# Stores of the up projection on the GpSimd queue, chunks of act in three pieces, the last normalisations in stages

## The chip, the cores and the metric

The kernel runs on one core of a Trainium2 chip. The metric is the device time of one execution in microseconds; less is better. The engines are TensorE (PE, matmul), VectorE (DVE), ScalarE (ACT) and GpSimd (POOL); SP is the queue that issues most DMAs.

## The reference

One layer of a hybrid encoder over 2048 tokens of width 1024, in float32: four mixers on a common input projection, an output projection with a residual and a layer normalisation, then a gated MLP with a causal convolution over 3 tokens, again with residual and normalisation. The change lies in the MLP and the last normalisation.

```python
def conv_ffn(h, w_up, conv_w, conv_b, w_down):            # D_FF = 2816
    u, gate = jnp.split(h @ w_up, 2, axis=-1)
    u = jax.nn.gelu(causal_dwconv(u, conv_w, conv_b))
    return (u * gate) @ w_down
...
    h = layer_norm(DN_ALPHA * h + y @ w_out[l], ln1_g[l], ln1_b[l])
    h = layer_norm(DN_ALPHA * h + conv_ffn(...), ln2_g[l], ln2_b[l])
```

## The kernel before

Every float32 operand of a matmul is split in a high and a low part, and a product is three matmuls: high by high (line 145), high by low (146 or 147) and low by high. The split of a tile is a cast on ScalarE (line 105) and a subtraction on VectorE (line 108). In the MLP the products of 2 by 2 blocks are taken as seven products of sums of blocks (numbered 1 to 7) in place of eight.

**Output projection** (`phase_o`): 16 tiles of 128 tokens. The layer normalisation of a tile (`layer_norm`, lines 80 to 94) runs over VectorE (statistics 85, 87, 91, product with the gain 93), GpSimd (reciprocal root 77 and 78, sum with the bias 94) and ScalarE (92); line 187 transposes the result on TensorE, lines 199, 200 and 219 are other work of GpSimd there.

**Up projection** (`phase_u`): 44 units, `fb` (half of the tokens) by `f` (128 of the 2816 channels), seven products of 12 matmuls each. In the first half the weights `wr` and their sums are stored in DRAM (`keep_sums`, line 1473, `su_d`, four a unit) and read back in the second half. `down_sums` makes sums of the down projection's weights and stores them (line 1505, `wt_d`). `activate` makes the convolution, the GELU and the gate (lines 1517 to 1523, tile `cv`, two buffers) and after each second unit four sums of blocks (`S`, one buffer), and stores `cv` and `S` to `ad_d`, 14 stores of 128 KB a pair of units (line 1537). All these stores are issued from SP, which also issues the loads of the weights.

**Down projection** (`phase_d`): the seven products in the order `DNO` (1, 6, 2, 5, 3, 7, 4), each over four chunks of act, 28 chunks in all. `load_b` loads the 11 weight tiles of a product (`dbr`, three buffers, line 1624; or straight into `db`) and splits them. `load_a` loads a chunk of act, 128 x 2816 (`da`, two buffers, 1408 KB, line 1632), and splits it as a whole, one chunk ahead of its use. A chunk gives two tiles of 33 matmuls; line 1674 adds the result to `accx` or `accy`. A tile of the output is complete with product 3 (`accx`) or 4 (`accy`): `residual` adds the residual (line 1639, `hres`), `finish` normalises in `layer_norm` and stores. For even tiles line 94 is on GpSimd, for odd ones on VectorE (`FL2`).

The instructions of each engine are put in order at build time by a scheduler that goes by the order of the code and by when buffers come free; on the chip each engine and each queue runs its own list in that order, and a waiting instruction holds up all that stand behind it.

Of the kernel before, what the change touches and what calls it, by code (L numbers as in the profile page):

```python
# [17 lines left out]
D = 1024  # L18
# [19 lines left out]
def r32(ap):  # L38
    return ap.bitcast(F32)
# [1372 lines left out]
def phase_u(K_, early):  # L1412
# [22 lines left out]
    with tc.tile_pool(name="uw", bufs=1, reuse_waits="tile", side="right") as ww, \  # L1435
# [35 lines left out]
        def keep_sums(n):  # L1471
            for q, i in enumerate((6, 5, 7, 3)):
                nc.sync.dma_start(K_.su_d[units[n][1], q], raws[n][i])

# [17 lines left out]
        def down_sums(j):  # L1492
            t = w.tile([128, 8, 256], F32, tag="wds", bufs=1, name="wds")
            for c in range(0, 512, 256):
                if c:
                    t = w.tile([128, 8, 256], F32, tag="wds", bufs=1, name="wds")
                for e in range(2):
                    nc.sync.dma_start(t[:, 2 * e:2 * e + 2], w_dn[j, e][:, :, c:c + 256])
                b11, b12, b21, b22 = (t[:, n] for n in range(4))
                t1, t2, t3, t4 = (t[:, 4 + n] for n in range(4))  # L1500
                V(t1, b12, b11, op=ALU.subtract)
                V(t2, b22, t1, op=ALU.subtract)
                V(t3, b22, b12, op=ALU.subtract)
                V(t4, b21, t2, op=ALU.subtract)
                nc.sync.dma_start(K_.wt_d[:, :, j, c:c + 256].rearrange("t p c -> p t c"), t[:, 4:8])
                yield
# [4 lines left out]
        def activate(n):  # L1511
# [13 lines left out]
            if f % 2:  # L1525
# [9 lines left out]
                for i, t in ((1, a11), (2, a12), (4, a22), (5, s1), (6, s2), (7, s3), (3, s4)):  # L1535
                    for c in range(2):
                        nc.sync.dma_start(K_.ad_d[i - 1, fb, c, :, j, :].rearrange("p (n c) -> p n c", c=128), t[:, 2 * c:2 * c + 2, :])

# [57 lines left out]
def phase_d(K_, out):  # L1596
# [12 lines left out]
    with tc.tile_pool(name="db", bufs=DBB, reuse_waits="tile") as wb, tc.tile_pool(name="dy", bufs=1, reuse_waits="tile") as cy, \  # L1609
# [19 lines left out]
        def load_a(i, fb, ch):  # L1629
            t = wa.tile([128, 2, NFP, 256], F32R, tag="da", name="da")  # L1630
            h, l = t[:, 0], t[:, 1]
            nc.sync.dma_start(r32(l), K_.ad_d[i - 1, fb, ch])
            K_.split(h, l, r32(l))
            return h, l

        def residual(ti, t):
# [3 lines left out]

        def finish(ti, t):
            K_.layer_norm(w, t, t, g2, b2, t, e2=nc.vector if FL2(ti) else None)
            nc.sync.dma_start(out[0, ti * 128:ti * 128 + 128, :], t)

# [9 lines left out]
        for s, (i, fb, ch) in enumerate(steps):  # L1654
# [7 lines left out]
            for t in range(2):  # L1662
# [16 lines left out]
                if i == 7:  # L1679
                    residual(ti + 1, y)  # L1680
                if i == 4:
                    finish(ti + 1, y)
            if later:
                ti, x = later.pop(0)
                residual(ti, x)
                finish(ti, x)

# [90 lines left out]
OBQ, OE2 = (lambda nc: nc.sync), (lambda nc, t: None)  # L1778
FL2 = lambda t: t % 2 == 1
FCB = 3  # L1780
# [37 lines left out]
```

## Time and profile before

| | |
|---|---|
| runs before | 3045.21 us median of 3 (3044.72 to 3049.33) |
| profiled execution | 3049.67 us, of which the span is 3047.9 us, mean granted TensorE clock 0.957 |
| busy share of the span | PE 92%, DVE 66%, ACT 41%, POOL 22% |
| instructions | PE 15515, DVE 3163, ACT 2017, POOL 534 |

The output projection runs from some 1495 to 1737 us of the profiled span, the up projection to 2580, the down projection from 2598 to 3034; the rest is the last normalisations. Busy shares are means over stages of very different kind, so each stage is read by itself.

### The profile page before, as it was taken

The numbers are of one execution on the slowest core, as the hardware profiler recorded it, in microseconds if no ns is written. First come the engines' busy times: TensorE is split into PE (matmuls) and PEld (weight loads), VectorE is DVE, ScalarE is ACT, GpSimd is POOL, SyncE is SP. The second block draws the span as 40 slices with busy tenths as digits, with TensorE's granted clock in tenths as the row PEclk, the third lists the DMA queues.
The fourth block names the chain that finished last, engine by engine and source line by source line (L and its number), as shares of the span: only waits on it lengthen the run. The fifth ranks groups of instructions, "written<-read, shape, count | busy, mean of one in ns | idle before, by whom it ended". The sixth has DMA issues, their size and how long they took to land. (4 is left out here: it accounts for less than half of the span.)

```text
span 3047.9 us, 42090 instructions
## 1 busy us (share of the span) xinstructions
PE 2793.5 (92%) x15515; PEld 2216.1 (73%) x15515; DVE 2013.2 (66%) x3163; ACT 1234.6 (41%) x2017; POOL 672.3 (22%) x534
## 2 busy tenths in 40 slices
PE   5899888999999877889888999999999998999997
PEld 3677766767677666777667788888888886788786
DVE  7877547555556286988866587787755556434666
ACT  3234233434433264555433354444644444332232
POOL 3433232222221252444445300000000000000111
PEclk8999997999999987999999999999999999999999
DMA  6566654646353456120566577775744443543462
GB/s 199 150 192 195 197 162 112 179 109 181 97 161 76 104 147 141 53 53 18 170 205 207 195 230 237 234 236 163 241 144 144 145 145 124 206 152 133 164 232 114
DMA packets 523757, 483.60 MB, mean 159 GB/s; under 512 B 100048, under 2 KB 432720, under 8 KB 517152
## 3 DMA queue, kind: packets, MB, share of 16 engines
q1 hardware_dynamic: 521584, 480.77, 51.8%
q8 instruction: 122, 2.00, 0.3%
q14 instruction: 83, 0.68, 0.1%
q10 hardware_dynamic: 1744, 0.14, 0.0%
q0 software_dynamic: 224, 0.01, 0.0%
HBM read 310.18 MB, written 170.64 MB: 158 GB/s over the span
## 5 line engine op out<-in xcount | busy, mean ns | idle before, releaser
L145 PE MATMUL u_ps<-bh,wh 128*128 128x512 f32 x1232 | 482.7, 392 | 6.2 <-ACT g L1581 3.2
L146 PE MATMUL u_ps<-bl,wh 128*128 128x512 f32 x1232 | 482.0, 391 | 0.0
L147 PE MATMUL u_ps<-bh,wl 128*128 128x512 f32 x1232 | 480.0, 390 | 0.6 <-DVE wl L1482 0.6
L137 POOL TENSOR_TENSOR wcl<-wraw,wch 128x512 fp32r<-128x512 f32 (+1 forms) x152 | 247.5, 1639 | 448.1 <-ACT wch L134 416.2
L1481 ACT CAST wh<-wr 128x512 fp32r<-128x512 f32 x308 | 189.7, 620 | 314.9 <-PE u_ps L146 270.6
L77 POOL TENSOR_SCALAR rsq_t<-ln_mv 128x1 f32<-128x1 f32 x48 | 19.2, 401 | 1334.2 <-DVE ln_mv L87 1293.1
L1482 DVE TENSOR_TENSOR wl<-wr,wh 128x512 fp32r<-128x512 f32 x308 | 210.8, 689 | 118.6 <-ACT wh L1481 118.6
L145 PEld LDWEIGHTS u_ps<-bh,wh 128*128 128x128 f32 x1232 | 231.5, 188 | 60.4 <-ACT g L1581 6.5
L147 PEld LDWEIGHTS u_ps<-bh,wl 128*128 128x128 f32 x1232 | 231.6, 188 | 51.7 <-DVE wl L1482 1.5
L146 PEld LDWEIGHTS u_ps<-bl,wh 128*128 128x128 f32 x1232 | 231.9, 188 | 47.8
L496 POOL TENSOR_TENSOR be<-be,af 128x512 f32<-128x512 f32 (+3 forms) x120 | 170.6, 1434 | 215.6 <-DVE af L494 129.3
L134 ACT CAST wch<-wraw 128x512 fp32r<-128x512 f32 (+1 forms) x152 | 110.2, 731 | 261.6 <-PE m L146 135.5
L145 PE MATMUL m<-hT,wch 128*128 128x512 f32 x448 | 190.3, 426 | 3.6 <-ACT wch L134 2.5
L147 PE MATMUL m<-hT,wcl 128*128 128x512 f32 x448 | 184.9, 413 | 2.6 <-POOL wcl L137 2.6
L146 PE MATMUL m<-hT,wch 128*128 128x512 f32 x448 | 184.6, 413 | 0.0
L494 DVE TENSOR_TENSOR_SCAN af<-sb_stay,af,sb_zero 128x513 f32<-128x513 f32 x96 | 137.6, 1450 | 7.3 <-ACT sb_stay L487 5.8
L146 PE MATMUL m<-hTl,wch 128*128 128x512 f32 x320 | 130.0, 406 | 8.1 <-POOL hTl L299 6.9
L145 PE MATMUL m<-hTh,wch 128*128 128x512 f32 x320 | 127.2, 404 | 6.9 <-DVE rw_halo L333 6.9
L105 ACT CAST da<-da 128x2816 fp32r<-128x2816 f32 x28 | 71.5, 2554 | 147.5 <-DMA da<-ad_d 141.7
L487 ACT ACTIVATE sb_stay<-a 128x512 f32<-128x512 f32 (+3 forms) x160 | 86.3, 539 | 110.8 <-PE a L483 63.5
L147 PE MATMUL m<-hTh,wcl 128*128 128x512 f32 x320 | 126.7, 396 | 0.0
L503 PE MATMUL b<-ident,be 128*128 128x128 f32 x544 | 92.6, 294 | 35.8 <-DVE wt L508 28.4
(516 smaller groups left out, 6383.5 us busy)
## 6 DMA issues: line engine op xcount, KB each, us to landing
wr<-in_ffn_w_up_dram SPq DMA_DIRECT2D x154, 256.0 KB
da<-ad_d SPq DMA_DIRECT2D x28, 1408.0 KB
wraw<-in_w_in_dram SPq DMA_DIRECT2D x112, 256.0 KB
su_d<-wr SPq DMA_DIRECT2D x88, 256.0 KB
ad_d<-S SPq DMA_DIRECT2D x176, 128.0 KB
wr<-su_d SPq DMA_DIRECT2D x88, 256.0 KB
wraw<-in_w_in_dram SPq DMA_DIRECT2D x40, 512.0 KB
ad_d<-cv SPq DMA_DIRECT2D x132, 128.0 KB
```

The costliest lines, as they stand in the source:

```text
L105: nc.scalar.copy(hi, src)
L134: nc.scalar.copy(hi[:, kk, cs], raw)
L137: (lo_eng or nc.vector).tensor_tensor(lo[:, kk, cs], raw, r32(hi[:, kk, cs]), op=ALU.subtract)
L145: nc.tensor.matmul(ps, lh, rh, start=start and i == 0, stop=False, **kw)
L146: nc.tensor.matmul(ps, lh, rl, start=False, stop=False, **kw)
L147: nc.tensor.matmul(ps, ll, rh, start=False, stop=i == n - 1, **kw)
L487: nc.scalar.activation(r[:, ns], lgn, AF.Sigmoid, scale=-1.0)
L494: nc.vector.tensor_tensor_scan(af[:, back], r[:, back], zero.to_broadcast([128, n + 1]), p["af"][:, TB - p["n"]:TB - p["n"] + 1] if p else ...
L496: (nc.gpsimd if i % 4 in WPP else nc.vector).tensor_tensor(be[:, ns], be[:, ns], af[:, TB - n + 1:], op=ALU.mult)
L503: nc.tensor.transpose(p[:, j * 128:(j + 1) * 128], u["be"][:, TB - n + j * 128:TB - n + (j + 1) * 128], K_.ident)
L1481: nc.scalar.copy(h, r)
L1482: V(l, r, r32(h), op=ALU.subtract)
```

## The change

All stores of the up projection go from SP to the queue of GpSimd. `load_a` loads and splits a chunk in three pieces of 4, 4 and 3 weight rows of 256 columns (1024, 1024 and 768 columns). `finish` becomes a generator of four stages, one taken after each tile of matmuls (`turn`); its statistics are instructions of their own (`stats`), of which one half of a tile is taken as soon as that half is final; line 94's sum is always on VectorE (now line 1667), and the very last tile runs in two halves, its store too.

```diff
@@ -1470,7 +1470,7 @@
 
         def keep_sums(n):
             for q, i in enumerate((6, 5, 7, 3)):
-                nc.sync.dma_start(K_.su_d[units[n][1], q], raws[n][i])
+                nc.gpsimd.dma_start(K_.su_d[units[n][1], q], raws[n][i])
 
         def weight(n, i):
             if n >= N:
@@ -1502,7 +1502,7 @@
                 V(t2, b22, t1, op=ALU.subtract)
                 V(t3, b22, b12, op=ALU.subtract)
                 V(t4, b21, t2, op=ALU.subtract)
-                nc.sync.dma_start(K_.wt_d[:, :, j, c:c + 256].rearrange("t p c -> p t c"), t[:, 4:8])
+                nc.gpsimd.dma_start(K_.wt_d[:, :, j, c:c + 256].rearrange("t p c -> p t c"), t[:, 4:8])
                 yield
 
         acts, stores = [], []
@@ -1534,7 +1534,7 @@
                 V(s4, a12, s2, op=ALU.subtract)
                 for i, t in ((1, a11), (2, a12), (4, a22), (5, s1), (6, s2), (7, s3), (3, s4)):
                     for c in range(2):
-                        nc.sync.dma_start(K_.ad_d[i - 1, fb, c, :, j, :].rearrange("p (n c) -> p n c", c=128), t[:, 2 * c:2 * c + 2, :])
+                        nc.gpsimd.dma_start(K_.ad_d[i - 1, fb, c, :, j, :].rearrange("p (n c) -> p n c", c=128), t[:, 2 * c:2 * c + 2, :])
 
         for i in (1, 2):
             moving(i, 0)
@@ -1629,18 +1629,54 @@
         def load_a(i, fb, ch):
             t = wa.tile([128, 2, NFP, 256], F32R, tag="da", name="da")
             h, l = t[:, 0], t[:, 1]
-            nc.sync.dma_start(r32(l), K_.ad_d[i - 1, fb, ch])
-            K_.split(h, l, r32(l))
+            for j in range(0, NFP, 4):
+                js = slice(j, min(j + 4, NFP))
+                nc.sync.dma_start(r32(l[:, js]), K_.ad_d[i - 1, fb, ch, :, js])
+                K_.split(h[:, js], l[:, js], r32(l[:, js]))
             return h, l
+
+        sts = {}
+
+        def stats(ti, t, q):
+            if ti not in sts:
+                sts[ti] = w.tile([128, 2, 6], F32, tag="ln_st", bufs=10, name="ln_st")
+            nc.vector.bn_stats(sts[ti][:, q, :], t[:, q * 512:(q + 1) * 512])
 
         def residual(ti, t):
             h = w.tile([128, D], F32, tag="hres", bufs=3, name="hres")
             nc.sync.dma_start(h, K_.h1_d[ti * 128:ti * 128 + 128, :])
             STT(t, h, ALPHA, t, op0=ALU.mult, op1=ALU.add)
 
-        def finish(ti, t):
-            K_.layer_norm(w, t, t, g2, b2, t, e2=nc.vector if FL2(ti) else None)
-            nc.sync.dma_start(out[0, ti * 128:ti * 128 + 128, :], t)
+        def finish(ti, t, last=False):
+
+            mv = w.tile([128, 2], F32, tag="ln_mv", bufs=3, name="ln_mv")
+            nc.vector.bn_aggr(mv, sts.pop(ti))
+            rs = w.tile([128, 1], F32, tag="ln_rs", bufs=3, name="ln_rs")
+            K_.rsqrt(w, rs, mv[:, 1:2], LN_EPS)
+            yield
+            nm = w.tile([128, 1], F32, tag="ln_nm", bufs=3, name="ln_nm")
+            STT(nm, mv[:, 0:1], -1.0, rs, op0=ALU.mult, op1=ALU.mult)
+            hs = [slice(0, 512), slice(512, D)] if last else [slice(0, D)]
+            for q in hs:
+                nc.scalar.activation(t[:, q], t[:, q], AF.Identity, scale=rs, bias=nm)
+            yield
+            for q in hs:
+                V(t[:, q], t[:, q], g2[:, q], op=ALU.mult)
+            yield
+            for q in hs:
+                V(t[:, q], t[:, q], b2[:, q], op=ALU.add)
+                nc.sync.dma_start(out[0, ti * 128:ti * 128 + 128, q], t[:, q])
+
+        run = []
+
+        def turn(new=None):
+
+            for r in list(run):
+                if next(r, 0) == 0:
+                    run.remove(r)
+            if new is not None:
+                next(new)
+                run.append(new)
 
         Bn = load_b(DNO[0])
         An = load_a(DNO[0], 0, 0)
@@ -1678,12 +1714,20 @@
                     later.append((ti, x))
                 if i == 7:
                     residual(ti + 1, y)
+                    stats(ti + 1, y, 1)
                 if i == 4:
-                    finish(ti + 1, y)
-            if later:
-                ti, x = later.pop(0)
-                residual(ti, x)
-                finish(ti, x)
+                    stats(ti + 1, y, 0)
+                    turn(finish(ti + 1, y, s + 1 == len(steps) and t))
+                elif t and later:
+                    ti, x = later.pop(0)
+                    residual(ti, x)
+                    stats(ti, x, 0)
+                    stats(ti, x, 1)
+                    turn(finish(ti, x))
+                else:
+                    turn()
+        while run:
+            turn()
 
 
 @with_exitstack
@@ -1776,7 +1820,6 @@
 
 
 OBQ, OE2 = (lambda nc: nc.sync), (lambda nc, t: None)
-FL2 = lambda t: t % 2 == 1
 FCB = 3
 DBB = 17
 QSTEP = 5
```

In the new listing line 1632 (load of `da`) is 1634, 1638 and 1639 are 1647 and 1648, 1643 (store of the output) is 1668, and 1674 is 1710; of the last normalisations 85 is 1643 (`stats`), 87 is 1653, 91 is 1658, 92 is 1661, 93 is 1664.

The SP queue at the end of the up projection, where the difference of the two orders is shown (`ad_d` is act in DRAM, `cv` and `S` the last unit's tiles, `dbr` the first weights of the down projection):

```order
-L1537 DMA ad_d<-cv 128x2x128 x2
-L1537 DMA ad_d<-S 128x256 x2
-L1632 DMA da<-ad_d 128x2816 x2
-L1537 DMA ad_d<-cv 128x2x128 x4
-L1537 DMA ad_d<-S 128x256 x6
-L1638 DMA hres<-h_d 128x1024 x2
+L1634 DMA da<-ad_d 128x1024 x2
+L1634 DMA da<-ad_d 128x768
+L1634 DMA da<-ad_d 128x1024 x2
+L1634 DMA da<-ad_d 128x768
+L1647 DMA hres<-h_d 128x1024 x3
 L1624 DMA dbr<-in_ffn_w_down_dram 128x512 x3
```

The stores are gone, and the loads of two chunks and three residuals stand directly ahead of the first `dbr`.

VectorE at the same place, from the last sum of products of the up projection on, before the change:

```order
L1578 TENSOR_TENSOR u<-u,u_ps 128x4x128
L1519 SCALAR_TENSOR_TENSOR cv<-u,ffn_cw,cv 128x1024 x2
L1523 TENSOR_TENSOR cv<-cv,g 128x1024
L1531 TENSOR_TENSOR S<-cv 128x512
L1532 TENSOR_TENSOR S<-S,cv 128x512
L1534 TENSOR_TENSOR S<-cv,S 128x512
L108 TENSOR_TENSOR da<-da 128x2816 x2
L108 TENSOR_TENSOR db<-dbr,db 128x512 x11
```

And in the changed kernel:

```order
L1578 TENSOR_TENSOR u<-u,u_ps 128x4x128
L1519 SCALAR_TENSOR_TENSOR cv<-u,ffn_cw,cv 128x1024 x2
L108 TENSOR_TENSOR da<-da 128x1024
L1523 TENSOR_TENSOR cv<-cv,g 128x1024
L108 TENSOR_TENSOR da<-da 128x1024
L1531 TENSOR_TENSOR S<-cv 128x512
L108 TENSOR_TENSOR da<-da 128x768
L1532 TENSOR_TENSOR S<-S,cv 128x512
L108 TENSOR_TENSOR da<-da 128x1024
L1534 TENSOR_TENSOR S<-cv,S 128x512
L108 TENSOR_TENSOR da<-da 128x1024
L108 TENSOR_TENSOR da<-da 128x768
```

The splits of two chunks, which followed the last unit's work as two instructions, are now six, put between its steps.

GpSimd in the output projection, where the first stores of the up projection come into its queue, before the change (`h` is a tile of the stream, `T` a sum of blocks):

```order
L199 TENSOR_TENSOR T<-hr 128x512
L77 TENSOR_SCALAR rsq_t<-ln_mv 128x1
L78 TENSOR_TENSOR ln_rs<-rsq_t,mhalf 128x1
L200 TENSOR_TENSOR T<-hr,T 128x512
L94 TENSOR_TENSOR h<-h,ln_b 128x1024
L219 TENSOR_TENSOR h<-h,ln_in_g 128x1024
```

And in the changed kernel:

```order
L199 TENSOR_TENSOR T<-hr 128x512
L77 TENSOR_SCALAR rsq_t<-ln_mv 128x1
L78 TENSOR_TENSOR ln_rs<-rsq_t,mhalf 128x1
L1473 DMA su_d<-wr_14924 128x512
L1473 DMA su_d<-wr_14923 128x512
L200 TENSOR_TENSOR T<-hr,T 128x512
L219 TENSOR_TENSOR h<-h,ln_in_g 128x1024
L94 TENSOR_TENSOR h<-h,ln_b 128x1024
L1473 DMA su_d<-wr_14922 128x512
L1473 DMA su_d<-wr_14925 128x512
```

Two stores now stand ahead of line 200, and lines 219 and 94 have changed places.

## Rows read from the trace of the kernel before

**Rows 1.** the windows of the whole core by stretch; x is the count.
```profile
core 0: us, PE busy (x) PEld busy (x) DVE busy (x) ACT busy (x) POOL busy (x), PEclk, DMA share, GB/s
1750.00:2570.00 820.00, 817.41 (x3580) 671.55 (x3579) 574.59 (x821) 379.71 (x634) 0.00 (x0) 1.00 0.60 186
2570.00:2600.00 30.00, 10.67 (x42) 7.88 (x41) 21.07 (x19) 13.32 (x12) 0.00 (x0) 0.73 0.66 238
...
2860.00:2900.00 40.00, 35.08 (x141) 27.82 (x140) 29.35 (x33) 9.98 (x6) 14.29 (x13) 0.91 0.54 190
2900.00:2995.00 95.00, 95.00 (x421) 78.69 (x420) 68.84 (x80) 31.33 (x28) 14.10 (x14) 1.00 0.57 207
2995.00:3010.00 15.00, 12.21 (x47) 9.57 (x46) 11.76 (x14) 3.65 (x2) 1.48 (x4) 0.89 0.44 169
```

**Rows 2.** the waits of TensorE (PE) from 2500 us to the end.
```profile
PE m L145 <- ACT db L105: 18.7, 1, 18.7
PE a L147 <- DVE da L108: 4.1, 2, 2.8
PE m L147 <- DVE da L108: 3.5, 1, 3.5
```

**Rows 3.** the timeline of the SP queue around the last unit.
```profile
2586.37 2.06 SPq L1537 DMA_DIRECT2D ad_d<-cv  x4
2588.53 3.06 SPq L1537 DMA_DIRECT2D ad_d<-S  x6
...
2592.64 1.42 SPq L1624 DMA_DIRECT2D dbr<-in_ffn_w_down_dram  x3
```

**Rows 4.** the chain that ended last, at the start of the down projection.
```profile
2593.11 4.90 DMA dbr<-in_ffn_w_down_dram
```

**Rows 5.** the timeline of VectorE (DVE) around the last unit.
```profile
2585.12 1.22 DVE L1523 TENSOR_TENSOR cv<-cv,g 128x1024 f32<-128x1024 f32 x1 [1.12 <-ACT cv L1522]
2586.38 0.69 DVE L1531 TENSOR_TENSOR S<-cv 128x512 f32<-128x512 f32 x1
...
2588.63 3.09 DVE L108 TENSOR_TENSOR da<-da 128x2816 fp32r<-128x2816 f32 x1
...
2597.99 2.05 DVE L108 TENSOR_TENSOR db<-dbr,db 128x512 fp32r<-128x512 f32 x3 [2.88 <-ACT db L105]
```

**Rows 6.** the stores on the SP queue, by their lines; durations in ns.
```profile
L1473 SPq DMA_DIRECT2D su_d<-wr x88: 319/332/663, 1528.2 to 2113.1; - x88
...
L1505 SPq DMA_DIRECT2D wt_d<-wds x22: 367/434/456, 1767.8 to 2049.5; - x22
...
L1537 SPq DMA_DIRECT2D ad_d<-S x176: 319/432/732, 1779.5 to 2591.1; - x176
L1537 SPq DMA_DIRECT2D ad_d<-cv x132: 366/462/1438, 1778.3 to 2587.9; - x132
```

**Rows 7.** DMAs that GpSimd (POOL) issues, line 376.
```profile
L376 POOL DMA_DIRECT2D ml_cw<-in_ml_conv_w_dram x4: 747/761/1030, 345.0 to 347.5; - x4
```

**Rows 8.** the timeline of GpSimd where its idle time ends.
```profile
2856.33 0.48 POOL L77 TENSOR_SCALAR rsq_t<-ln_mv 128x1 f32<-128x1 f32 x1 [1120.35 <-DVE ln_mv L87]
```

**Rows 9.** the ends of the timelines of TensorE and of VectorE.
```profile
3033.36 0.39 PE L147 MATMUL c<-db,da 128*128 128x512 f32 x1
...
3030.59 0.68 DVE L1674 TENSOR_TENSOR accy<-accy,m 128x512 f32<-128x512 f32 x1
...
3037.56 0.68 DVE L1674 TENSOR_TENSOR accy<-accy,c 128x512 f32<-128x512 f32 x1
...
3042.93 1.23 DVE L94 TENSOR_TENSOR accy<-accy,ln_b 128x1024 f32<-128x1024 f32 x1
```

**Rows 10.** the waits of TensorE in the output projection, 1495 to 1745 us.
```profile
PE a L187 <- POOL h L94: 30.5, 9, 5.2
```

**Rows 11.** the timeline of GpSimd in the output projection.
```profile
1550.56 2.35 POOL L94 TENSOR_TENSOR h<-h,ln_b 128x1024 f32<-128x1024 f32 x1 [2.63 <-DVE h L93]
1552.86 2.35 POOL L219 TENSOR_TENSOR h<-h,ln_in_g 128x1024 f32<-128x1024 f32 x1
```

## The prediction, made before the change was run

> **What bounds the kernel now.** I read the windows first, stage by stage. While the up projection runs, TensorE is busy for 817.4 of 820 us and nothing around it can be won; then come 30 us of which it works 10.7 us, at the change from up to down projection, and two shorter holes late in the down projection, 40 us with 35.1 busy and 15 us with 12.2 busy [rows 1]. The waits of TensorE name the causes: once 18.7 us for the first cast weight of the down projection (`db`, line 105), three times, 7.6 us together, for the low half of a chunk of act (`da`, line 108) [rows 2]. So the kernel is bound by TensorE, and the change can earn time only in these holes, and behind TensorE's last matmul.
>
> The SP queue shows why the big hole is so long. Its first `dbr` load is issued at 2592.64, straight behind ten stores of the last unit, issued one after the other from 2586.37 to 2591.59 [rows 3]; the chain of waits follows it for 4.90 us until the data lie in SBUF [rows 4]. The stores themselves wait for VectorE's product at 2585.12 [rows 5]. A load that needs nothing of them stands in line behind stores that came late.
>
> **The queue of the stores.** 418 stores leave SP: 88 + 22 + 176 + 132, of 0.33 to 0.43 us each there [rows 6]. On GpSimd the trace has only seven tiny DMAs; four of them took 0.75 to 1.03 us to issue [rows 7]. A unit is 84 matmuls; at 3580 in 820 us [rows 1] that is 19.24 us, and a pair takes 38.5 us. In the first half of the phase a pair has 8 + 14 + up to 3 = 25 stores, in the second 14. From below: 25 x 0.33 = 8 us, from above 25 x 1.03 = 26 us, both under 38.5. GpSimd did nothing for 1120 us before 2856 [rows 8], so I put the move at nothing while the up projection runs; the limit is 38.5 / 25 = 1.54 us a store. Past it `cv`, `S` and `wr`, which are freed only by these stores, come late, and the weights with them. At 1.03 us the stores of `cv` and `S` of the pair before are out long before the last unit wants the buffers.
>
> The rows say about 1 us. The Trainium skill, page "SBUF — State Buffer", section "A bandwidth-pool intuition that's wrong (but worth ruling out)", speaks against the move: a DMA issued from GpSimd that takes about 620 ns alone takes about 3100 ns beside a VectorE copy that holds the shared port, and the page advises to issue from ACT or SP. By that price, an estimate from the page, 24 stores would be 74 us a pair and the kernel some 450 us slower. No row here shows a DMA of GpSimd beside VectorE's work of this phase, which is sums and products of two tensors and no copy.
>
> **The change from up to down.** In the new order of SP the six loads of `da` and three of `hres` stand ahead of `dbr`, and no store. They wait for TensorE's last products alone, so `dbr` goes out at about 2579.4 + 3 x 0.41 = 2580.7, 12 us earlier. Behind the three `hres` loads it is 2.4 MB; at 238 GB/s with a DMA share of 0.66 [rows 1], 360 GB/s at full use, that takes 6.6 us, so the data lie there by about 2589. That is not worth 9 us, because VectorE is late next: in its new order the six pieces of `da` are split between the steps of the last unit and before the first `db`. From the rows [rows 5]: its second `cv` step ends at 2584.0 (2585.12 less the wait of 1.12 before it); then the pieces, 1024 columns at 1.22 (the 128x1024 product), 768 at 0.95 (between 0.69 and 1.22), so 2 x 3.39 us, the product 1.22 and the three sums of `S` at 0.72 each. 2584.0 + 6.78 + 1.22 + 2.16 = 2594.1 for the first `db` split, where it was 2597.99. **Gain 3.9 us.** Bounds: nothing, if the DMA engines deliver `dbr` only by 2597; 6 us, if VectorE fills its waits better. TensorE stands still long enough in either case to restart at the lower clock, so that part cancels.
>
> **The chunks in three pieces.** At the two late holes one split of 3 us and more [rows 5] came to its turn when TensorE already wanted it. Counted in matmuls, at the 0.2257 us of the undisturbed 95 us with 421: 40 us should hold 177 and held 141, 15 us should hold 66.5 and held 47 [rows 1]; that is 8.2 + 4.4 = 12.6 us, 7.6 of it waiting and the rest at the granted clock of 0.91 and 0.89, the lower level after each wait (a few records may be missing, so it is an upper end). In the new order of VectorE each of these chunks is split in pieces that stand ahead of the sum for the next tile, not behind it and its residual; worked through with the row durations, the first piece is ready 3 to 9 us before TensorE wants it. VectorE gets 8 sums of 1.22 us from GpSimd (line 94 of the even tiles) and some 0.3 us a chunk for the extra instructions. The added issues on SP, two a chunk at 0.33, lie under 15 us of matmuls a chunk. **Gain 11 us**, less than the count for the missing records, between nothing (VectorE's order again puts a piece late) and 12.6.
>
> **Statistics early, last normalisations in stages.** TensorE's last matmul starts at 3033.36 and takes 0.39; VectorE adds its result at 3037.56 only, 3.8 us late, because the previous tile's normalisation, 6.97 us from add to add, stands ahead of it [rows 9]. In the new order it still stands ahead; but one statistics instruction of 0.69 a tile is gone from there, so a tile takes about 6.4 us where TensorE takes 33 x 0.2257 = 7.45, and the last chunk's split stands before the first of the four tiles. Late by about 2 us at the first, VectorE has caught up at the last: 3.5 us. The last tile in halves saves some 0.2 us of its 6.6 us chain and perhaps 0.5 us of the last store, which carries half the bytes. **Gain 4.2 us**, between 1 (the tile before still stands in the way) and 6. That the statistics are early counts little: one half was taken early already.
>
> **What it costs.** The stores of the first two units fall into the output projection, where GpSimd works and TensorE waits 30.5 us for its line 94 [rows 10]. In the new order two stores and line 219 stand ahead of one line 94 that started at 1550.56: 2 x 0.75 + 2.35 = 3.9 us at most [rows 7, 11], partly given back because line 219 is then done. **Loss 2.5 us** (0 to 5).
>
> **Sum.** 3.9 + 11 + 4.2 - 2.5 = 16.6 us. Against the profiled execution, 3049.67 us, that is 3033; it lies 4.5 us above the median of the runs, 3045.21, which two of three runs agree on. From the median: 3028.6, and I say 3029.
>
> **Rivals.**
> 1. One large term fails (chance 0.18): a piece is late again and the holes stay, or the `dbr` loads are held up by the DMA engines, whose share is 0.66 in that stretch. 3032 to 3040.
> 2. Most of it fails, or the stores cost the output projection more, within 0.2% (6 us, about what a measurement of this kernel can tell from no change), chance 0.12: about 3042. For it speaks that VectorE is busy 29.4 of 40 us where the holes are [rows 1], and gets more work there.
> 3. Slower, 0.10: the GpSimd queue is the bound of the first half of the up projection. From 1.54 us a store each 0.1 us more costs 25 x 0.1 x 11 pairs = 27 us, so from 1.62 us the kernel is slower than before by over 0.2%, and 2 us a store gives 3029 + 11 x (50 - 38.5) = 3155 us. For it: most stores are of 128 KB and more, where the DMAs of the rows moved 2 KB, and nothing shows how the issue grows with the size. Against it, four rows at 0.75 to 1.03 us. It is what the page of the Trainium skill named above would lead to.
>
> The forecast itself has 0.60, with 3022 to 3036 as its own range. Faster by over 0.2%: 0.60 + 0.17 = 0.77; within 0.2%: 0.13; slower: 0.10. The range from 3019 to 3044 leaves out the slow rival and some of the ends.
>
> **What would show it.** First `dbr` issue some 12 us before the place where it was, VectorE and not a DMA ahead of TensorE's restart, the wait at 14 to 15 us where it was 18.7; no wait for `da` over 1 us in the down projection; VectorE's last add within 0.5 us of the last matmul; stores on GpSimd at most 1.1 us each. The forecast is wrong if TensorE waits inside the up projection, if a new wait for `da` appears, or if the output projection loses over 5 us.

## The result, and the profile after

The changed kernel takes 3063.93 us (median of 4 runs, 3059.1 to 3068.48), the kernel before in the same comparison 3046.72 us (4 runs). The ratio is 1.0052, 95% interval 1.0036 to 1.0068: 0.5% slower, where 3029 us and a gain were forecast. The profiled execution has a span of 3064.8 us, 16.9 us more than before. Cut at the starts of the first and the last matmul of each phase, in us:

| | up projection starts | up projection | hole to the first matmul of the down projection | down projection | behind it |
|---|---|---|---|---|---|
| before | 1722.3 | 856.7 | 19.0 | 435.4 | 14.5 |
| after | 1724.9 | 889.9 | 11.0 | 425.4 | 13.6 |
| difference | +2.6 | **+33.2** | -8.0 | -10.0 | -0.9 |
| forecast | +2.5 | **0** | -3.9 | -11 | -4.2 |

Four terms came out with the sign forecast, and together they are 16.3 us of gain, against 16.6. That the sums agree so well is luck: the gain at the hole is twice the forecast, the one behind the last matmul a fifth of it. The one that had been put at nothing took 33.2 us. Windows of the whole core (columns as in [rows 1]), before and then after:

```profile
1750.00:2150.00 400.00, 397.41 (x1738) 325.49 (x1737) 317.14 (x487) 184.81 (x321) 0.00 (x0) 1.00 0.71 224
```
```profile
1750.00:2150.00 400.00, 375.56 (x1595) 305.89 (x1595) 295.36 (x458) 168.21 (x292) 137.64 (x228) 0.97 0.63 209
1750.00:2570.00 820.00, 795.01 (x3434) 651.09 (x3434) 558.87 (x800) 368.65 (x615) 232.44 (x382) 0.99 0.58 185
```

All of it lies in the first half of the phase. There TensorE did 1595 matmuls where it had done 1738; 143 at 0.2257 us are 32.3 us. It was busy for 375.56 us against 397.41, so 21.9 us of it are waits; the other 10 us go with the lower granted clock, 0.97 where it was 1.00 (the last section shows one such place). In the second half it did 1839 (3434 less 1595) against 1842 (3580 of [rows 1] less 1738). What each engine waited for from 1745 to 2150, before:

```profile
PE u_ps L145 <- ACT g L1581: 2.5, 5, 1.2
...
DVE wr L1466 <- DMA wr<-in_ffn_w_up_dram: 32.3, 12, 3.6
...
DVE wds L1501 <- DMA wds<-in_ffn_w_down_dram: 8.6, 7, 1.7
...
SPq L1459 <- DVE wl L1482: 37.3, 29, 4.7
SPq L1498 <- DMA wt_d<-wds: 25.8, 15, 3.2
```

And after:

```profile
PE u_ps L145 <- ACT g L1581: 24.4, 8, 4.8
...
DVE wds L1501 <- DMA wds<-in_ffn_w_down_dram: 56.8, 14, 5.5
DVE wr L1466 <- DMA wr<-in_ffn_w_up_dram: 20.1, 12, 2.7
...
SPq L1459 <- DVE wl L1482: 203.5, 63, 10.9
SPq L1498 <- DMA wt_d<-wds: 103.1, 21, 8.2
```

VectorE's wait for the up projection's own weights `wr` fell, from 32.3 to 20.1 us: these do not come late. SP stands longer at their loads (line 1459), 203.5 us for 37.3, but has no stores left to issue in that time; in run 14 it stands there for 179.3 us and nothing is lost. TensorE waits for ScalarE, which waits for VectorE, which stands at line 1501, the first sum of a piece of `down_sums`, for the weights of that piece. These weights are loaded into `wds`, a tile with one buffer; the load (line 1498) waits until the store of the piece before has read the tile out. So there is a ring: load, sums, store, next load. The chain that ended last, in the changed kernel, runs straight through it (start, us, what):

```profile
1865.23 4.36 DMA wt_d<-wds
...
1869.61 3.09 DMA wds<-in_ffn_w_down_dram
...
1872.79 0.09 DVE wds L1501
...
1874.42 0.60 DVE wl L1482
1875.02 0.61 DVE u L1578
...
1876.81 0.60 ACT wh L1481
1877.41 0.49 ACT g L1581
```

VectorE's timeline at this place:

```profile
1862.19 0.42 DVE L1504 TENSOR_TENSOR wds<-wds 128x256 f32<-128x256 f32 x1
1862.53 1.89 DVE L1482 TENSOR_TENSOR wl<-wr,wh 128x512 fp32r<-128x512 f32 x3
1866.64 0.69 DVE L1466 TENSOR_TENSOR wr<-wr,wr 128x512 f32<-128x512 f32 x1 [2.22 <-DMA wr<-in_ffn_w_up_dram]
1872.79 0.43 DVE L1501 TENSOR_TENSOR wds<-wds 128x256 f32<-128x256 f32 x1 [5.46 <-DMA wds<-in_ffn_w_down_dram]
```

Between the last sum of one piece, done at 1862.6, and the first of the next stand four instructions, 2.6 us of work. The ring needs 10.2 us: the store is issued at 1865.23, lands 4.4 us later, and the load takes 3.1. So VectorE stands still for 7.7 us, 2.2 of them for the load of `wr` and 5.5 for the piece, and behind it in its list stand the split of the next weights and the sum from which `g` and the next products follow; TensorE resumes at 1877.94 after 3.8 us of waiting.

The store is issued 2.6 us after the last sum here, behind two stores of `S` and 1.55 us in which GpSimd stood idle. That is one of the worst places: over the last 18 turns of the ring this leg takes 0.9 us in the mean (0.5 before), and from the store's issue to the reload's issue it is 4.1 us (4.0 before). So the way over GpSimd makes the ring only 0.6 us longer a turn. What changed more is the work that VectorE has in that time: where twelve instructions stand between two pieces, the 9.5 to 10.8 us from the last sum to the next first one pass without a wait; where seven stand, as in the changed kernel at every third piece, 9.3 us hold a wait of 4.4. At the places with four, the wait is 3.8, and was 1.5 before (medians).

GpSimd's stores are not slow. The same lines as [rows 6], with the queue changed (ns, shortest/median/longest):

```profile
L1537 POOL DMA_DIRECT2D ad_d<-S x176: 542/550/564, 1782.9 to 2628.0; - x176
L1537 POOL DMA_DIRECT2D ad_d<-cv x132: 708/720/740, 1781.4 to 2624.6; - x132
L1473 POOL DMA_DIRECT2D su_d<-wr x88: 542/542/684, 1530.9 to 2148.4; - x88
L1505 POOL DMA_DIRECT2D wt_d<-wds x22: 762/762/771, 1784.0 to 2094.3; - x22
```

Where the forecast hoped to gain, the turn from up to down first. The waits of TensorE, which answer to [rows 2]:

```profile
PE m L145 <- ACT db L105: 10.6, 1, 10.6
PE m L146 <- DVE db L108: 3.4, 2, 3.2
```

SP issues the first `dbr` directly behind the residuals, and VectorE reaches the first split of `db` through the pieces ([rows 3] and [rows 5] are the places before; the first line is the last matmul of the up projection):

```profile
2614.77 0.39 PE L147 MATMUL u_ps<-bh,wl 128*128 128x512 f32 x1
...
2616.31 2.34 SPq L1624 DMA_DIRECT2D dbr<-in_ffn_w_down_dram  x3
```
```profile
2627.01 2.09 DVE L108 TENSOR_TENSOR da<-da 128x1024 fp32r<-128x1024 f32 x2
2629.01 1.89 DVE L108 TENSOR_TENSOR db<-dbr,db 128x512 fp32r<-128x512 f32 x3
```

No wait for `da` is left in the down projection. At the end of the program the sums of the last four tiles (line 1710, as line 1674 in [rows 9]), and the last matmuls of the same tiles:

```profile
3031.43 3.22 DVE L108 TENSOR_TENSOR da<-da 128x1024 fp32r<-128x1024 f32 x3
3034.57 0.68 DVE L1710 TENSOR_TENSOR accy<-accy,a 128x512 f32<-128x512 f32 x1
...
3048.64 0.68 DVE L1710 TENSOR_TENSOR accy<-accy,m 128x512 f32<-128x512 f32 x1
3055.16 0.68 DVE L1710 TENSOR_TENSOR accy<-accy,c 128x512 f32<-128x512 f32 x1
```
```profile
3028.72 0.39 PE L147 MATMUL a<-db,da 128*128 128x512 f32 x1
...
3043.68 0.39 PE L147 MATMUL m<-db,da 128*128 128x512 f32 x1
3051.16 0.39 PE L147 MATMUL c<-db,da 128*128 128x512 f32 x1
```

### The profile page after: what moved, and what is told of

It reads as the page before. It is cut to its first block, busy times and chain, and to the rows that moved or that the text cites. A ratio compares the mean times of both kernels' runs of the same rounds, so it can differ in the third digit from the quotient of the medians.

```text
span 3064.8 us, 42412 instructions
## 1 busy us (share of the span) xinstructions
PE 2809.5 (92%) x15515; PEld 2227.4 (73%) x15515; DVE 2027.2 (66%) x3229; ACT 1244.0 (41%) x2074; POOL 908.7 (30%) x944
## 5 line engine op out<-in xcount | busy, mean ns | idle before, releaser
L137 POOL TENSOR_TENSOR wcl<-wraw,wch 128x512 fp32r<-128x512 f32 (+1 forms) x152 | 248.1, 1643 | 450.0 <-ACT wch L134 418.6
L1537 POOL DMA_DIRECT2D ad_d<-cv x132 | 94.2, 719 | 481.1 <-DVE cv L1523 477.1
L108 DVE TENSOR_TENSOR da<-da 128x1024 fp32r<-128x1024 f32 (+1 forms) x84 | 92.6, 1131 | 82.3 <-ACT da L105 82.1
L105 ACT CAST da<-da 128x1024 fp32r<-128x1024 f32 (+1 forms) x84 | 79.6, 977 | 146.5 <-DMA da<-ad_d 144.7
```

The costliest lines, as they stand in the source:

```text
L108: nc.vector.tensor_tensor(lo, src, r32(hi), op=ALU.subtract)
L137: (lo_eng or nc.vector).tensor_tensor(lo[:, kk, cs], raw, r32(hi[:, kk, cs]), op=ALU.subtract)
L1537: nc.gpsimd.dma_start(K_.ad_d[i - 1, fb, c, :, j, :].rearrange("p (n c) -> p n c", c=128), t[:, 2 * c:2 * c + 2, :])
```

## The experiments

Theory R: the ring of `wds`. Moving stores from SP changes the order that the scheduler gives to VectorE in the first half, so that the sums of a piece stand too close behind the store of the one before; the in-order VectorE waits there, and all behind it. Rival Q: the queue of GpSimd; stores stand there in one line behind others that wait for VectorE, so `cv`, `S` and `wr` come free late.

The table has all runs: the phases as above, VectorE's wait at the sums of the pieces and TensorE's for `g` from 1745 to 2150, and the number of VectorE's instructions, in the built order, from one piece's last sum to the next one's first, over three pieces. The ratio is that to the kernel before in the same comparison; run 5 has two executions only. Profiled executions differ by up to 16 us before the up projection starts, in code that no version changes; phases are the better comparison where totals lie close.

| stores on GpSimd | ratio, 95% interval | up | hole | down | tail | VectorE wait | TensorE wait | instructions between |
|---|---|---|---|---|---|---|---|---|
| none (before) | 1 | 856.7 | 19.0 | 435.4 | 14.5 | 8.6 | 2.5 | 4+12+12 |
| all (after) | 1.0052, 1.0036 to 1.0068 | 889.9 | 11.0 | 425.4 | 13.6 | 56.8 | 24.4 | 4+12+7 |
| 1: all but `wt_d` | 1.0019, 1.0 to 1.0039 | 878.4 | 10.9 | 425.4 | 14.7 | 74.2 | 15.3 | 4+5+12 |
| 2: `wt_d` alone, on before | 1.0072, 1.0044 to 1.0099 | 870.3 | 19.2 | 435.1 | 14.4 | 21.5 | 12.9 | 7+5+9 |
| 3: all, sums in a tile of their own | 1.0065, 1.0045 to 1.0085 | 897.9 | 11.0 | 425.4 | 14.8 | 66.5 | 27.5 | 1 to 10, mean 4 |
| 4: none, rest as after | 0.997, 0.9954 to 0.9985 | 856.3 | 21.9 | 422.8 | 16.1 | 10.2 | 1.9 | 4+12+12 |
| 5: all, on before | 1.0087, 1.006 to 1.0115 | 885.8 | 11.6 | 438.7 | 14.9 | 55.5 | 24.9 | 4+12+7 |
| 6: all, three of four sums held, one piece a unit | 1.0114, 1.0092 to 1.0136 | 911.2 | 11.0 | 428.6 | 14.5 | 100.4 | 34.0 | one sum not held |
| 7: none, `da` in pieces alone, on before | 1.0007, 0.9992 to 1.0023 | 853.3 | 22.5 | 427.7 | 19.9 | 7.9 | 0.2 | 4+12+12 |
| 8: act of the second half | 0.9926, 0.9902 to 0.995 | 854.4 | 10.9 | 425.4 | 15.1 | 9.3 | 0.9 | 4+12+12 |
| 9: act of the last four units | 0.9958, 0.9934 to 0.9981 | 854.9 | 11.0 | 425.5 | 15.8 | 9.6 | 1.4 | 4+12+12 |
| 10: all, three of four sums held in the second half | 1.0085, 1.006 to 1.0111 | 889.6 | 23.3 | 426.4 | 14.3 | no sums there | 1.2 | one sum not held |
| 11: all, no loads and sums of pieces | 1.0012, 0.9994 to 1.003 | 870.7 | 11.0 | 428.1 | 14.2 | no sums | 11.3 | |
| 12: all but `su_d` | 0.9957, 0.9934 to 0.9981 | 862.1 | 11.0 | 425.7 | 15.7 | 24.1 | 5.1 | 4+12+12 |
| 13: all, four sums held in the second half | 0.9981, 0.9964 to 0.9999 | 854.9 | 22.0 | 427.2 | 13.5 | no sums there | 1.2 | 13 a piece |
| 14: all, four sums held, one piece a unit | 0.9952, 0.9932 to 0.9971 | 856.1 | 11.0 | 429.5 | 13.9 | none | 2.6 | 14 to 17 a piece |

**1. `wt_d` back on SP.**

```diff
-                nc.gpsimd.dma_start(K_.wt_d[:, :, j, c:c + 256]...
+                nc.sync.dma_start(K_.wt_d[:, :, j, c:c + 256]...
```

> The changed kernel, with the 22 stores of the weight sums (line 1505) issued from SP again; the other 396 stores stay on GpSimd. Theory R (ring): the up projection lost 33 us because VectorE stands in line for the reload of `wds`, whose one buffer is free only when its store has landed; the store from GpSimd lands after 3.8 us and the reader stands earlier in VectorE's order. Then VectorE's wait for `wds` falls from 57 us to under 20, TensorE's 24 us of waits in the up projection to under 8, and the time to 3030 to 3040 us. Rival L (late weights): the stores of `su_d` and `ad_d` free `wr`, `cv` and `S` too late; then the up projection stays at 890 us and the time over 3055 us.

3050.83 us, which neither theory has, and Theory R's waits were missed as well. Of the 33 us only 11.5 came back, and VectorE waits longer at the ring than before the edit, 74.2 us, although the stores are on SP again. So the price is not one of the queue that these 22 stores take; the order had become tighter still, 21 instructions in three pieces. TensorE loses less than after all the same, so the count of instructions alone does not give the size.

**2. `wt_d` alone on GpSimd, on the kernel before.** The same line, moved the other way, on the kernel before.

> The kernel before, with the 22 stores of the weight sums alone issued from GpSimd. Theory R: the up projection loses 20 to 35 us and the whole kernel takes 3066 to 3080 us. Rival L: nothing is late, 3042 to 3052 us.

3066.51 us: moving 22 of 418 stores to an empty queue costs 13.6 us in the up projection. Two of its waits from 1745 to 2150:

```profile
DVE wds L1501 <- DMA wds<-in_ffn_w_down_dram: 21.5, 12, 5.4
...
POOL wt_d L1505 <- DVE wds L1504: 313.3, 22, 32.1
```

GpSimd stands idle before each of them until the sums are done: nothing queues there. That cannot be Q, and speaks for R, though the 13.6 us lie under its 20 to 35. The medians differ by 20.5 us, more than the phases tell, because the profiled execution is the fastest of the four (3062.72 us) and the one of the kernel before lay above its median.

**3. The sums in a tile of their own**, so that a reload no longer waits for a store.

```diff
-            t = w.tile([128, 8, 256], F32, tag="wds", bufs=1, name="wds")
+            t, o = (w.tile([128, 4, 256], F32, tag=g, bufs=1, name=g) for g in ("wds", "wts"))
-                t1, t2, t3, t4 = (t[:, 4 + n] for n in range(4))
+                t1, t2, t3, t4 = (o[:, n] for n in range(4))
```

> The changed kernel, all stores on GpSimd, but the four sums of down_sums lie in a tile of their own (same memory in all), so that a reload waits for VectorE's sums and not for the store. Theory R: VectorE's wait for `wds` under 20 us, the up projection some 860 to 868 us long, the time 3030 to 3042 us. Rival L: as the changed kernel, 3058 to 3070 us.

A miss: 3066.95 us, up projection 897.9. The wait only changed its name, from the reload to the store that must have read the sums' tile:

```profile
DVE wts L1501 <- DMA wt_d<-wts: 66.5, 18, 6.8
```

The scheduler used the freedom to put the pieces closer still. The cut had moved to another leg of the ring and cost no less.

**4. All stores on SP**, the pieces of `da` and the staged normalisations kept: the three `gpsimd` of the diff set back to `sync`.

> The changed kernel with all 418 stores on SP: the pieces and the staged normalisations alone. The stores then cost the up projection nothing. If the 18 us that the down projection won came 8 from the SP queue at its start and 10 from the pieces, this takes 3034 to 3038 us; if the pieces win alone what was predicted for them (11) and the normalisations 4.2, 3031 us; if the pieces win only together with the free SP queue, 3044 to 3048 us.

3037.96 us: the up projection is as before, the hole 2.9 us longer (21.9). So those two parts alone gain 8 us between the medians, and the move of the stores has both its 33 us of loss and 11 us of gain at the hole, of which the down projection gives 2.6 back.

**5. The move alone**, on the kernel before: the three lines set to `gpsimd`.

> The kernel before with all 418 stores on GpSimd and nothing else changed. Theory R: up projection 33 us longer, hole at the down projection's start 8 to 11 us shorter, rest as before: 3066 to 3076 us. If the pieces or the staged normalisations have a part in the loss, under 3060 us.

3076.29 us, 0.3 us above R's range: up projection +29.1, hole -7.4 and down projection +3.3. The loss needs nothing of the rest of the change; the built order round the pieces is that of the changed kernel.

**6. Pieces held to one a unit**: the sums in a tile of their own, the pieces in the first half, each behind a copy of one column of the unit's `cv` into its first sum.

```diff
+                nc.vector.tensor_copy(o[:, 0, 0:1], gate[0][:, 0:1])
-                if units[n - 1][0]:
+                if not units[n - 1][0]:
```

> The changed kernel, all 418 stores on GpSimd, but the weight sums are paced: one piece a unit in the first half of the up projection, its sums in a tile of their own and tied by a one-column copy behind the unit's `cv`, so that 19 us lie between two pieces and no reload or store is late. Theory R, as the runs so far narrow it (what costs is that VectorE's order, made at build time, puts the next piece's sums so near behind the store that VectorE waits there, whichever queue stores): VectorE's wait at the weight sums under 5 us, the up projection 856 to 862 us, the time 3028 to 3038 us. Rival G (stores from GpSimd are slow by themselves and hold `cv`, `S` and `wr`): the up projection stays over 875 us and the time over 3050 us.

A miss, the worst of all: 3084.92 us. The edit did not do what it was for. The third sum (line 1504 there, `b22` less `b12`) needs nothing of the first, and the scheduler put it straight behind the piece before:

```profile
1880.55 0.42 DVE L1505 TENSOR_TENSOR wts<-wds,wts 128x256 f32<-128x256 f32 x1
1880.88 1.28 DVE L1482 TENSOR_TENSOR wl<-wr,wh 128x512 fp32r<-128x512 f32 x2
1889.25 0.43 DVE L1504 TENSOR_TENSOR wts<-wds 128x256 f32<-128x256 f32 x1 [7.08 <-DMA wds<-in_ffn_w_down_dram]
```

One sum of 0.43 us at the wrong place in an in-order list makes VectorE stand still for 7 us. The numbers are those that Rival G wanted; the lines above show VectorE waiting at the ring and not for `cv`, `S` or `wr`.

**7. `da` in pieces alone**, on the kernel before: `load_a` as in the diff, nothing else.

> The kernel before with the chunks of act loaded and split in three pieces and nothing else changed. If the 10 us that the down projection won come from the pieces: 3034 to 3040 us, no wait of TensorE for `da` over 1 us. If they come from the staged normalisations (statistics early, line 94 on VectorE): 3043 to 3049 us, with the waits for `da` still there.

3049.82 us, no difference. The down projection is 7.7 us shorter, but the hole 3.5 us and the end 5.4 us longer: without the staged normalisations VectorE ends later. The two parts earn together (run 4) what the pieces alone do not; the staged normalisations alone were not run.

**8. The first half's stores on SP**, only the act stores of the second half on GpSimd.

```diff
-                        nc.gpsimd.dma_start(K_.ad_d[...
+                        (nc.gpsimd if fb else nc.sync).dma_start(K_.ad_d[...
```

with `su_d` and `wt_d` on `sync`.

> The changed kernel with the stores of the first half (`su_d`, `wt_d`, `ad_d` of the first tokens) on SP and only the `ad_d` stores of the second half on GpSimd. Theory R: the first half is as with all stores on SP (up projection 856 us), and the start of the down projection has its free SP queue (hole of 11 us in place of 19 to 22): 3026 to 3033 us. Rival G: the second half, with 14 stores a pair on GpSimd, loses some 10 us: 3036 to 3045 us.

3027.42 us against 3047.95, faster than both kernels and close to the 3029 forecast, which had nothing for the failed step. The window, as [rows 1]:

```profile
1750.00:2150.00 400.00, 399.15 (x1749) 327.82 (x1748) 320.63 (x489) 189.46 (x327) 0.00 (x0) 1.00 0.72 228
```

**9. Only the last four units' act stores on GpSimd**: as run 8, with `fb and f >= NFF - 4`.

> The changed kernel with all stores of the up projection back on SP, but for the act stores of the last two pairs of units (28 of 418), which stay on GpSimd. The order of VectorE in the first half is that of before. Theory R (the reload ring of wds, made tight by the new order in the first half, cost the 33 us; what the change earns at the turn from up to down comes only from the last unit's stores being off SP): up projection 853 to 858 us, hole 11 us, total 3024 to 3033 us, like the version with the whole second half on GpSimd (3027.4). Rival Q (the gain of that version comes from SP being free of stores in the whole second half): hole 17 to 22 us as with all stores on SP, total 3034 to 3040 us.

3035.78 us, 3 us above R's range and inside Q's, but the phases are those of run 8 to 0.7 us: hole 11.0, where Q had 17 to 22. The 14 us between the two profiled executions lie before the up projection starts (1727.0 against 1712.7). So 28 stores bring the whole gain of the move.

**10. The pieces held in the second half**, all stores on GpSimd.

```diff
+                nc.vector.tensor_copy(t1[:, 0:1], gate[0][:, 0:1])
                 V(t1, b12, b11, op=ALU.subtract)
```

`gate[0]` is the unit's `cv`; the code makes the pieces in the second half, and the scheduler had drawn them into the first.

> The changed kernel, all 418 stores on GpSimd, with one added instruction per piece: a copy of one column of the unit's cv into the piece's first sum, ahead of the sums. It holds the pieces in the second half, where the code has them and from where the scheduler had drawn them into the first; 20 to 30 instructions of VectorE then stand between two pieces. Theory R: the waits of VectorE for wds in the first half go away, up projection 853 to 862 us, total 3026 to 3037 us. Rival Q (the in-order queue of GpSimd with all the stores of the first half is itself the cause, by holding cv and the weights wr): up projection 875 us or more, total 3050 us or more.

The total, 3071.46 us, and the up projection, 889.6, are those of Q, a miss for R, and the halves of the phase tell why:

```profile
1750.00:2150.00 400.00, 398.78 (x1750) 328.06 (x1749) 294.89 (x400) 190.38 (x322) 129.43 (x220) 1.00 0.52 170
...
2150.00:2570.00 420.00, 401.78 (x1722) 327.55 (x1721) 263.33 (x406) 183.76 (x301) 99.45 (x158) 0.98 0.59 189
```
```profile
DVE wds L1504 <- DMA wds<-in_ffn_w_down_dram: 106.8, 17, 10.3
```

In the first half, with its stores of `su_d` and act on GpSimd, TensorE does 1750 matmuls, more than before the change; that VectorE has no sums of pieces there helps it too. In the second half, where the ring now is, it does 1722 instead of 1842, and the last line, a wait of VectorE from 2150 to 2570, names the third sum, which was not held here either. The loss went with the ring and not with the stores of `cv`, `S` and `wr`. The hole is 23.3 us for the reason given at run 13.

**11. No loads and no sums of pieces**, 22 stores of zeros from one tile, all stores on GpSimd.

```diff
-                for e in range(2):
-                    nc.sync.dma_start(t[:, 2 * e:2 * e + 2], w_dn[j, e][:, :, c:c + 256])
...
-                nc.gpsimd.dma_start(K_.wt_d[:, :, j, c:c + 256]..., t[:, 4:8])
+                nc.gpsimd.dma_start(K_.wt_d[:, :, j, c:c + 256]..., zt)
```

> The changed kernel without the work of down_sums: its loads and its sums are left out, and the 22 stores to wt_d go out from a tile of zeros, still from GpSimd among all the others (so the output is not the reference's). No ring is left, the stores are all there. Theory R: up projection 850 to 860 us, total 3022 to 3035 us. Rival Q (queue): the waits stay, up projection 870 us or more, total 3045 us or more. VectorE has 88 sums of some 0.4 us less to do, some 33 us in 425, which helps under either theory and is why this run does not stand alone.

870.7 us for the up projection and 3049.55 in all, over R's ranges and just inside Q's. The edit has a flaw: the 22 stores of zeros need nothing from VectorE and are all issued at the start, from 1739 to 1804, 11 MB, and the loads of `wr` come late once, 7.5 us. Behind that TensorE waits no more:

```profile
1750.00:1800.00 50.00, 37.34 (x150) 29.00 (x149) 29.66 (x39) 21.91 (x33) 15.15 (x23) 0.86 0.96 350
...
1800.00:2150.00 350.00, 350.00 (x1537) 288.30 (x1536) 254.00 (x348) 159.58 (x277) 117.86 (x200) 1.00 0.50 162
```

50 us hold 221 matmuls and held 150, 16 us lost in one stretch at a DMA share of 0.96; after it come 350 us without a gap, with the stores of `su_d` and act on GpSimd.

**12. `su_d` back on SP**, the other 330 stores on GpSimd. The built order round the pieces is then that of before.

```diff
-                nc.gpsimd.dma_start(K_.su_d[units[n][1], q], raws[n][i])
+                nc.sync.dma_start(K_.su_d[units[n][1], q], raws[n][i])
```

> The changed kernel with only the 88 stores of su_d back on SP; wt_d and all stores of act, 330, stay on GpSimd. The build-time order of VectorE round the pieces is then that of before (4, 12 and 12 instructions between one piece's last sum and the next one's first, where the changed kernel has 4, 12 and 7). Theory R, with the order as the cause of the tight ring: up projection 855 to 863 us, total 3027 to 3038 us. Rival Q (the stores of pieces stand on GpSimd behind act stores that wait for VectorE, whatever the order): up projection 870 us or more, total 3043 us or more.

3034.45 us, as R has it; up projection 862.1, 27.8 us less than after. The wait at the ring is 24.1 us where it was 56.8, TensorE's 5.1 where it was 24.4. Two things changed here, the order and that no `su_d` store stands ahead of `wt_d`; run 14 keeps the `su_d` stores there.

**13. As run 10, with all four sums held.**

```diff
+                nc.vector.tensor_copy(t3[:, 0:1], gate[0][:, 0:1])
```

> As the run that held the pieces in the second half, with all 418 stores on GpSimd, but with a second copy of one column of cv, into the third sum. In that run and in the one that held the pieces to one a unit, the third sum (b22 less b12) needed nothing of the gated tile, and stood straight behind the piece before, where VectorE waited for it up to 10 us each time. Now all four sums of a piece come one unit, some 19 us, after those of the piece before. Theory R (a ring too short for its turn-around): no waits for wds over 1 us in the middle of the phase, up projection 852 to 862 us, hole 11 to 16 us, total 3026 to 3038 us. Rival Q (GpSimd's queue): up projection 870 us or more.

3042.06 us, over R's range. The up projection is whole (854.9), but the hole is 22.0 us, where R had 11 to 16. The ring is now at work until the end of the phase, and its last reload stands on SP ahead of `dbr`, which goes out 9.7 us after the last matmul started, 1.5 in the changed kernel:

```profile
2571.81 1.21 SPq L1498 DMA_DIRECT2D wds<-in_ffn_w_down_dram  x2
...
2575.97 2.12 SPq L1628 DMA_DIRECT2D dbr<-in_ffn_w_down_dram  x3
```

**14. The same in the first half**: run 13 with `if not units[n - 1][0]`.

> The same with the pieces in the first half, one a unit, where the changed kernel had them. All 418 stores on GpSimd, the same loads, sums and bytes as the changed kernel; only the sums' place in VectorE's order differs, with 13 to 20 instructions between two pieces. Theory R: up projection 853 to 863 us, hole 11 us, total 3026 to 3038 us, so some 25 to 35 us faster than the changed kernel. Rival Q: up projection 870 us or more, TensorE's waits for g 10 us or more from 1745 to 2150 us.

3030.06 us against 3048.18. The window, and from 1745 to 2150 us the longest wait of VectorE and the one of SP for the ring:

```profile
1750.00:2150.00 400.00, 397.42 (x1742) 326.68 (x1742) 320.37 (x519) 189.40 (x323) 144.25 (x240) 1.00 0.68 222
```
```profile
DVE wl L1482 <- ACT wh L1481: 51.2, 38, 2.1
...
SPq L1498 <- DMA wt_d<-wds: 96.1, 19, 8.3
```

All 418 stores are on GpSimd, with the same bytes, loads and sums as in the changed kernel, in the same half; two copies of one column a piece fix the place of the sums, and the 33 us are gone. SP still waits 96 us for the stores to land, where it was 103; VectorE waits no longer for a piece, since its list has other work in that time. The ring itself is even longer: from the last sum of a piece to the issue of the next load it takes 6.7 us in the mean, 5.0 in the changed kernel and 4.5 before. So the way over GpSimd costs nothing where the ring has room, and Q falls. The down projection is 4 us longer than after, which stays unexplained.

## Why the prediction was wrong

- **Failed: "so I put the move at nothing while the up projection runs", limit 1.54 us a store.** The price of a store was right, 0.54 to 0.76 us, at most half the limit. The step asked only whether the queue can carry the stores. What moved was a leg of a ring: `wt_d` and the reload of `wds` share one buffer, and VectorE, in order, does the sums between them. And the built order of VectorE changed in the first half, which the prediction had looked at only from the turn from up to down on. The text lists `cv`, `S` and `wr` as freed by these stores and leaves out `wds`, whose stores stand in [rows 6]. With 4+12+7 instructions between pieces in place of 4+12+12, and a ring 0.6 us longer a turn, VectorE's waits went from 8.6 to 56.8 us, TensorE's from 2.5 to 24.4, and with the lower clock 33.2 us were lost. That the place of the sums is the cause is shown by run 14, which keeps every store on GpSimd and moves the sums alone. That a tight order does it without GpSimd in the ring is in run 1. With before's order, `wt_d` on GpSimd and `su_d` off it, 24.1 us of VectorE's wait and 5.4 us of the loss are left (run 12), so some of the wait comes from the longer way and not from the order; before's order with all 418 stores on GpSimd was not run. Why the scheduler orders so stays open.
- **Rival 3** had the right stage and the wrong mechanism. It wanted 1.62 us a store. The Trainium skill, page "SBUF — State Buffer", section "A bandwidth-pool intuition that's wrong (but worth ruling out)", would have about 3100 ns for a DMA that GpSimd issues beside a VectorE copy. Here no store held GpSimd for over 0.77 us with VectorE busy 295 of 400 us; from issue to landing a store of `cv` or `S` took 2.1 to 6.7 us, 3.5 in the median. VectorE's work there was sums and products of two float32 tensors, so the page's own case, a copy, is not tried by this.
- **The turn from up to down**: right in its mechanism, no DMA ahead of TensorE any more, and too small. Ahead of the first matmul it is ScalarE, which casts five pieces of `da` up to 2625.2 before the first `db`; ahead of the second it is VectorE, as forecast. `dbr` goes out at 2616.31, 1.5 us after the last matmul started (2614.77), the first `db` split comes at 2629.01. The hole fell by 8.0 us, 3.9 forecast. But TensorE's second matmul waits another 3.2 us for VectorE, so until it runs on the gain is 4.8 us (the second matmul starts 14.6 us after the last product, 19.4 before; the first needs no split). Against run 4, where the pieces are there and the stores on SP, the move gives 10.9, or 7.7 counted to the second matmul.
- **The pieces**: 10.0 us, 11 forecast. Counted from the second matmul, as the hole above, it is 13.2, over the bound of 12.6. All waits of TensorE for `da` are gone. But alone the pieces give nothing in total (run 7); the gain needs the staged normalisations beside them (run 4).
- **The end**: mis-sized, 0.9 us for 4.2. The rate was right: 6.52 us a tile on VectorE where TensorE takes 7.48. But VectorE starts 5.5 us late (3034.57 against 3029.11), not 2, because the three pieces of the last chunk still stand ahead of the first sum, and it catches up in the last two steps only, by 0.95 us each; at the last it is 3.6 late, 3.8 before.
- **The output projection**: +2.6, 2.5 forecast. But TensorE's wait there fell a little against [rows 10] (the same view, after), where it was to grow:

```profile
PE a L187 <- POOL h L94: 27.3, 8, 8.9
```

The start of the up projection varies by more than 2.6 us between executions, so this term was not measured, and that it agrees with the forecast is luck.

## What to carry to other kernels

When a store changes its queue, look for what its landing sets free: if it is a tile with one buffer that is loaded, worked on and stored, count the whole ring (issue of the store, landing, reload, arrival) against the work that the in-order engine has between two turns, and compare that engine's built order before and after through the whole stretch, not only where the gain is hoped for. A queue that is a third full can still cost time by what the ring behind it makes others wait for. Where the ring can't have a second buffer, fix the place of all its steps (run 14), or move only the stores that the gain needs: 28 of 418 brought the whole gain at the turn (run 9). A second buffer for `wds` was not tried.

## What the runs showed of the hardware

- A store issued from GpSimd took 0.54 to 0.55 us (`su_d`, 256 KB; `S`, 128 KB), 0.72 (`cv`, 128 KB) and 0.76 us (`wt_d`, 512 KB), so not in proportion to its bytes; on SP the same took 0.33 to 0.46 [rows 6]. The prediction had 0.75 to 1.03 on GpSimd and, misread by a little, 0.33 to 0.43 on SP.
- One burst of 22 independent stores, 11 MB at a DMA share of 0.96 and 350 GB/s, went with 16 us lost by TensorE in 50 us, while loads of weights came late (run 11); no other run tries the burst by itself.
- TensorE's wait of 3.8 us that ends at 1877.94 is followed, after some matmuls at 0.39 us, by such of 0.54 and 0.63. In the 10 us round it the granted clock is 0.83, so a part at 1.2 GHz, and 24 matmuls ran where 44 fit; 2.9 us of the 10 are the wait:

```profile
1875.00:1885.00 10.00, 7.06 (x24) 5.64 (x25) 9.48 (x16) 5.99 (x11) 3.09 (x6) 0.83 0.69 226
```
